# Quarter loads, packed tiles and one full-width chain in place of two interleaved chunks, in a 4:8 sparsifying kernel

One core of one Trainium2 chip. The metric is the device time of one execution in microseconds (us). Most executions of a kernel agree within some 0.3 us; a run more than 1.5% above the fastest of the same kernel is called slow. Medians below are over all runs, ratios over the fast runs only.

## The reference

```python
batch, dim = 64, 4096                      # x: float32, normal
x_flat  = x.copy().reshape(-1, 8)
indices = np.argsort(np.abs(x_flat), axis=-1)
for i in range(x_flat.shape[0]):
    x_flat[i, indices[i, :4]] = 0          # the 4 smallest of 8 become 0
```

Every value keeps itself if its magnitude is among the four largest of its group of eight. The kernel doesn't sort. It finds the fourth largest magnitude of a group with a network of minima and maxima, compares the eight magnitudes with it and multiplies by the mask.

## The kernel before

The 64 x 4096 input is laid out as 128 partitions x 2048 values, that is 256 groups of eight per partition. It goes through in two chunks of 128 groups, each with tiles of its own (two buffers), so that the scheduler can put the second chunk's instructions between the first's:

```python
for c in range(2):                                   # NCHUNK
    nc.sync.dma_start(out=x_t, in_=x_v[:, col0:col1])            # 512 KB
    nc.scalar.activation(out=a, in_=x_t, func=Abs)               # ACT
    tt(hi1, ev, od, max); tt(lo1, ev, od, min)                   # level 1, 512 values each
    tt(Q[0:2], hi1 even, hi1 odd, max); tt(mh, ..., min)         # level 2, 4 ops of 256
    tt(nl, lo1 even, lo1 odd, max);     tt(U[3:5], ..., min)
    tt(Q[2:4], mh, nl, max); tt(Q[4:6], mh, nl, min)             # the mh/nl pair
    tt(U[0:3], Q[0::2], Q[5:0:-2], min)                          # the minimum, 384
    nc.vector.tensor_reduce(t4, U, max)                          # 640 -> 128
    tt(mask, a, t4 broadcast, is_ge); tt(res, mask, x_t, mult)   # 1024 each
    nc.scalar.dma_start(out=out_v[:, col0:col1], in_=res)        # 512 KB
# (shortened: tt is nc.vector.tensor_tensor, slices without the group axis)
```

## Time and profile before

| | before |
|---|---|
| median time | 25.09 us |
| span of the profile | 23.3 us |
| VectorE (DVE) starts | 5.73 us |
| last DVE op ends | 19.82 us |
| after it, to the end of the span | 3.48 us |

The change is judged by three lengths: the head (until DVE starts), the DVE stretch and the tail (after the last DVE op). ACT is ScalarE, which computes Abs; SP is SyncE, which issues the loads and at the end waits for the stores. A transfer has landed when its completion semaphore has arrived. Two more lines of the page of the kernel before are needed below. The first is a group of instructions (line, engine, operation, output<-inputs, shapes, count | busy us, mean ns of one | idle us before). The second is a DMA issue (KB each, us from issue to landing):

```profile
L84 DVE TENSOR_TENSOR U<-Q 128x384 f32<-128x384 f32 x2 | 1.3, 626 | 0.0
...
x_t<-in_x_dram SPq DMA_DIRECT2D x2, 512.0 KB, 4.3
```

### The profile page before, as it was taken

What the parts mean: (1) busy time and instruction counts of PE and PEld (TensorE: products, weight loads), DVE (VectorE), ACT (ScalarE), POOL (GpSimd) and SP (SyncE); (2) the same over time, 40 slices, a digit from 0 to 9 for tenths busy, and PEclk for the clock granted to TensorE, in tenths of its full rate; (3) what the DMA queues carried; (4) which work ended last, traced back from release to release, by engine and by line L of the source; (5) the groups of instructions that cost most, each with busy time, mean ns of one, the idle gap of its engine ahead of it and who ended that gap; (6) DMA issues with size and microseconds to landing.
All of it is one profiled execution on the core that took longest, in us unless ns stands there. A gap on an engine that the chain in (4) does not pass through costs nothing.

```text
span 23.3 us, 77 instructions
## 1 busy us (share of the span) xinstructions
DVE 14.0 (60%) x24; ACT 3.4 (15%) x3; POOL 0.2 (1%) x4
## 2 busy tenths in 40 slices
DVE  0000000001999999999999999999999999000000
ACT  0794000097980000000000000000000000000000
POOL 3000000000000000000000000000000000000000
DMA  0014979971000000000000000069500000059700
GB/s 0 0 14 113 323 211 373 408 302 56 0 0 0 0 0 0 0 0 0 0 0 0 0 0 0 0 274 401 225 0 0 0 0 0 0 211 401 288 0 0
DMA packets 576, 2.10 MB, mean 90 GB/s; under 512 B 64, under 2 KB 64, under 8 KB 576
## 3 DMA queue, kind: packets, MB, share of 16 engines
q1 hardware_dynamic: 288, 1.05, 13.4%
q10 hardware_dynamic: 288, 1.05, 11.1%
HBM read 1.05 MB, written 1.05 MB: 90 GB/s over the span
## 4 chain that ended last, share of the span: by engine, by line
DVE 59%; DMA 17%; ACT 5%; issue 2%
DMA x_t<-in_x_dram 17%; DVE mask L104 11%; DVE res L108 10%; DVE t L99 7%; DVE hi L59 6%; DVE lo L60 5%; DVE U L84 5%; ACT a_abs L49 5%; DVE U L77 3%; DVE Q L81 3%; DVE nl L74 3%; DVE mh L71 3%; DVE Q L80 3%; DVE Q L68 2%
## 5 line engine op out<-in xcount | busy, mean ns | idle before, releaser
L59 DVE TENSOR_TENSOR hi<-a_abs 128x512 f32<-128x512 f32 x2 | 1.4, 686 | 5.7 <-ACT a_abs L49 5.7
L49 ACT ACTIVATE a_abs<-x_t 128x1024 f32<-128x1024 f32 x2 | 2.1, 1056 | 2.8 <-DMA x_t<-in_x_dram 2.8
L108 DVE TENSOR_TENSOR res<-mask,x_t 128x1024 f32<-128x1024 f32 x2 | 2.5, 1225 | 0.0
L104 DVE TENSOR_TENSOR mask<-a_abs,t 128x1024 f32<-128x1024 f32 x2 | 2.4, 1224 | 0.0
L99 DVE TENSOR_REDUCE t<-U 128x128 f32<-128x640 f32 x2 | 1.6, 818 | 0.0
L49 ACT ACT_TABLE_LOAD x1 | 1.3, 1283 | 0.7 <-PEq L125 0.7
L60 DVE TENSOR_TENSOR lo<-a_abs 128x512 f32<-128x512 f32 x2 | 1.4, 687 | 0.0
L84 DVE TENSOR_TENSOR U<-Q 128x384 f32<-128x384 f32 x2 | 1.3, 626 | 0.0
L77 DVE TENSOR_TENSOR U<-lo 128x256 f32<-128x256 f32 x2 | 0.9, 440 | 0.0
L74 DVE TENSOR_TENSOR nl<-lo 128x256 f32<-128x256 f32 x2 | 0.8, 420 | 0.0
L81 DVE TENSOR_TENSOR Q<-mh,nl 128x256 f32<-128x256 f32 x2 | 0.8, 420 | 0.0
L68 DVE TENSOR_TENSOR Q<-hi 128x256 f32<-128x256 f32 x2 | 0.8, 419 | 0.0
L71 DVE TENSOR_TENSOR mh<-hi 128x256 f32<-128x256 f32 x2 | 0.8, 419 | 0.0
L80 DVE TENSOR_TENSOR Q<-mh,nl 128x256 f32<-128x256 f32 x2 | 0.8, 418 | 0.0
L125 POOL MEMSET const-bfloat16-1.0<- 128x1 bf16 x1 | 0.1, 102 | 0.0
L125 POOL MEMSET const-uint8-127<- 128x1 uint8 x1 | 0.1, 102 | 0.0
L125 POOL MEMSET const-float32-0.0<- 128x1 f32 x1 | 0.1, 99 | 0.2 <-issue 0.2
L125 POOL MEMSET const-float32-1.0<- 128x1 f32 x1 | 0.1, 99 | 0.0
## 6 DMA issues: line engine op xcount, KB each, us to landing
x_t<-in_x_dram SPq DMA_DIRECT2D x2, 512.0 KB, 4.3
out_dram<-res ACTq DMA_DIRECT2D x2, 512.0 KB, 2.7
```

Of the source, the lines that this page charges most:

```text
L49: nc.scalar.activation(out=a.rearrange("p g e -> p (g e)"), in_=x_t.rearrange("p g e -> p (g e)"), func=mybir.ActivationFunctionType.Abs,)
L59: nc.vector.tensor_tensor(out=hi1, in0=ev, in1=od, op=ALU.max)
L60: nc.vector.tensor_tensor(out=lo1, in0=ev, in1=od, op=ALU.min)
L71: nc.vector.tensor_tensor(out=mh, in0=hi1_r[:, :, :, 0], in1=hi1_r[:, :, :, 1], op=ALU.min)
L74: nc.vector.tensor_tensor(out=nl, in0=lo1_r[:, :, :, 0], in1=lo1_r[:, :, :, 1], op=ALU.max)
L77: nc.vector.tensor_tensor(out=U[:, :, 3:5], in0=lo1_r[:, :, :, 0], in1=lo1_r[:, :, :, 1], op=ALU.min)
L80: nc.vector.tensor_tensor(out=Q[:, :, 2:4], in0=mh, in1=nl, op=ALU.max)
L81: nc.vector.tensor_tensor(out=Q[:, :, 4:6], in0=mh, in1=nl, op=ALU.min)
L84: nc.vector.tensor_tensor(out=U[:, :, 0:3], in0=Q[:, :, 0::2], in1=Q[:, :, 5:0:-2], op=ALU.min)
L99: nc.vector.tensor_reduce(out=t4, in_=U, axis=mybir.AxisListType.X, op=ALU.max)
L104: fin.tensor_tensor(out=mask, in0=a, in1=t4.to_broadcast([P, G, 8]), op=ALU.is_ge)
L108: fin.tensor_tensor(out=res, in0=mask, in1=x_t, op=ALU.mult)
```

## The change

The intent: start DVE sooner, by loading in quarters and doing Abs and level 1 on each quarter; use fewer instructions, by packing the intermediate results into 8-word groups so that level 2 takes two ops in place of four and the rest runs once on all 256 groups; shorten the last store, by splitting the output 160 to 96.

```diff
-NCHUNK = 2
+IN_SEGS = [0, 64, 128, 192, 256]
+OUT_SEGS = [0, 160, 256]
 ...
+    for g0, g1 in zip(IN_SEGS[:-1], IN_SEGS[1:]):
+        nc.sync.dma_start(out=x_t[:, g0:g1, :], in_=x_v[:, g0:g1, :])
+        nc.scalar.activation(out=a[:, g0:g1, :], in_=x_t[:, g0:g1, :], func=Abs)
+        nc.vector.tensor_tensor(out=T1[:, g0:g1, 0:4], in0=ev, in1=od, op=ALU.max)
+        nc.vector.tensor_tensor(out=T1[:, g0:g1, 4:8], in0=ev, in1=od, op=ALU.min)
+    # from here on all 256 groups at once
+    tt(QQ words 0,1,6,7, T1 even, T1 odd, max); tt(W words 0,1,6,7, ..., min)
+    tt(QQ[2:4], W[0:2], QQ[6:8], max);          tt(QQ[4:6], ..., min)
+    tt(W[3:6], QQ[0:6:2], QQ[5:0:-2], min)
+    nc.vector.tensor_reduce(out=t4, in_=W[:, :, 3:8], op=max)
+    for g0, g1 in zip(OUT_SEGS[:-1], OUT_SEGS[1:]):
+        tt(mask, a, t4 broadcast, is_ge); tt(res, mask, x_t, mult)   # one mask buffer
+        nc.scalar.dma_start(out=out_v[:, g0:g1, :], in_=res[:, g0:g1, :])
 ... (removed: the loop over two chunks shown above; long calls shortened)
```

## The prediction

> **What bounds the kernel now.** I read the page of the profile first (busy shares and slices), then the chain of work that ended last, then the timeline, which gives the start of each single instruction.
>
> The page's busy shares, and the slices of 0.58 us:
>
> ```profile
> DVE 14.0 (60%) x24; ACT 3.4 (15%) x3; POOL 0.2 (1%) x4
> ...
> DVE  0000000001999999999999999999999999000000
> ...
> DMA  0014979971000000000000000069500000059700
> ```
>
> VectorE (DVE) is busy without a break from slice 9 to slice 33. Before that it has nothing to work on; after it only a transfer runs. So there are three parts: a head until DVE starts, a solid DVE stretch, and a tail with the last store.
>
> The timeline (start, duration, engine, line) at both ends of the DVE stretch:
>
> ```profile
> 4.64 1.06 ACT L49 ACTIVATE a_abs<-x_t 128x1024 f32<-128x1024 f32 x1 [2.63 <-DMA x_t<-in_x_dram]
> 5.73 0.69 DVE L59 TENSOR_TENSOR hi<-a_abs 128x512 f32<-128x512 f32 x1 [5.73 <-ACT a_abs L49]
> 5.85 1.06 ACT L49 ACTIVATE a_abs<-x_t 128x1024 f32<-128x1024 f32 x1 [0.15 <-DMA x_t<-in_x_dram]
> ...
> 15.03 0.42 DVE L80 TENSOR_TENSOR Q<-mh,nl 128x256 f32<-128x256 f32 x1
> 15.36 0.42 DVE L81 TENSOR_TENSOR Q<-mh,nl 128x256 f32<-128x256 f32 x1
> 15.82 0.63 DVE L84 TENSOR_TENSOR U<-Q 128x384 f32<-128x384 f32 x1
> 16.48 0.82 DVE L99 TENSOR_REDUCE t<-U 128x128 f32<-128x640 f32 x1
> 17.34 1.22 DVE L104 TENSOR_TENSOR mask<-a_abs,t 128x1024 f32<-128x1024 f32 x1
> 18.59 1.23 DVE L108 TENSOR_TENSOR res<-mask,x_t 128x1024 f32<-128x1024 f32 x1
> ```
>
> Read from it:
> - Load 1 has landed at about 4.62 us, load 2 at about 5.83 us (ACT starts 0.02 us later). DVE starts at 5.73.
> - Two neighbours that don't depend on each other (L80, L81) start 0.33 apart though one lasts 0.42: they overlap by some 0.08. An op that needs the result just before it (L84, L99, L104, L108) starts 0.03 after its end. A direct dependence thus costs about 0.115 us more than independence.
> - The last DVE op ends at 19.82; the span is 23.3. The tail is 3.48 us.
>
> The DMA part of the page gives the tail its content:
>
> ```profile
> out_dram<-res ACTq DMA_DIRECT2D x2, 512.0 KB, 2.7
> ```
>
> Issue to landing is 2.7 us for 512 KB. The windows of this store show 410 and 393 GB/s where it is in full flow, so about 1.3 us is bytes and 1.4 us is fixed; another 0.75 us of the span follows the landing. The median time (25.09) is 1.79 above the span, which I take as unchanged.
>
> **What the Trainium skill says.**
> - "VectorE: DVE Perf Modes", section "The TRN2 errata": an fp32 tensor_tensor takes (N+151)/0.96 ns. The groups agree: N=256 gives 424 (measured 419 to 420), 512 gives 691 (686), 1024 gives 1224 (1224 to 1225). I use it for 768 and 1280.
> - Same page, section "The DRAIN you can't avoid": a semaphore between chained ops costs nothing extra. The trace here differs, by the 0.115 us above, and I go by the trace.
> - "SBUF — State Buffer", section "Door 1: The DMA port swizzle": lines are 16 bytes, and at least two accesses in a row should hit the same line. The trace agrees: the stride-2 reads of L68 (two hits per line) show no penalty, while L84 measures 626 ns where the formula gives 557. Its reversed input (words 5, 3, 1 of a 6-word group) makes one single hit per group of 8 values on average: 128 of them for about 70 ns, or 0.55 ns each.
> - "ScalarE: Activation LUTs", section "What ACT_TABLE_LOAD costs": 0.833 ns per element. With the measured 1056 ns for 1024 elements, a 512-element Abs is estimated at 1056 - 427 = 629 ns.
>
> **The change, part by part.**
>
> *Instructions and elements.* The DVE elements per partition are the same: 2048 for level 1, 2048 for level 2, 1024 for the mh/nl pair, 768 for the minimum, 1280 for the reduce, 4096 for mask and multiply; 11,264 in all. DVE instructions fall from 24 to 18 (8 + 2 + 2 + 1 + 1 + 4). At about 70 ns of fixed pitch (0.33 us apart less 256/0.96 = 267 ns) this saves some 0.4 us. By itself that is under 2%.
>
> *What it loses.* The two chunks were interleaved so that a chunk-1 op stood between dependent chunk-0 ops. Now there is one chain on the whole width. Direct dependences: into level 2, the pair, the minimum, the reduce, mask 1, res 1, mask 2 (it reuses the one mask buffer) and res 2: eight, against five or so exposed before (L84, L99, L104, L108 and little else). Cost about +0.4 us, eating the saving in instructions.
>
> *Layout.* W[3:6] in 8-word groups straddles two lines, QQ[0,2,4] and QQ[5,3,1] likewise: each of three ports has one single hit in each of 256 groups. One port's worth is 256 x 0.55 = 140 ns; the ports overlap partly, so I choose +200 ns: 768 elements cost 957 + 200 = 1.16 us, against two at 0.626 before. The reduce (5 words starting at word 3) has one single hit per group; I choose +50 ns on 1333 + 152 = 1485 ns. The pair writes to words 0-1 and 6-7 sit whole in a line and cost nothing extra.
>
> *The head: where the gain is.* Before, DVE's 5.73 to 19.82 is all work. Now level 1 (8 ops, 0.34 apart, 2.7 us) runs as quarter loads of 256 KB land, most of it before the last byte is in. The last quarter should land when load 2 did, 5.85: same bytes, same queue, four issues of some 0.42 from 0.73 on are all out by 2.4. Then Abs 0.63 to 6.48, two level-1 ops 0.34 apart and 0.42 long, end at 7.26. For that the earlier quarters must be worked off: landings 0.65 to 0.7 apart (256 KB at some 400 GB/s) against 0.68 us of DVE and less than that of ACT; they just fit.
>
> *The chain from there* (start of the next = start + duration + 0.03 if dependent, - 0.08 if not):
>
>     7.29  level-2 max, 1024 elements, 1.224, next independent
>     8.43  level-2 min, 1.224
>     9.68  pair max, 512, 0.686, next independent
>     10.29 pair min, 0.686
>     11.00 minimum, 768, 1.16
>     12.19 reduce, 1280, 1.535
>     13.76 mask 1, 1280, 1.49
>     15.28 res 1, 1.49
>     16.80 mask 2, 768, 0.957
>     17.79 res 2, 0.957, ends 18.75
>
> So DVE ends 1.07 us earlier than 19.82.
>
> *The tail.* The last store falls from 512 to 384 KB: 128 KB at 410 GB/s is 0.31 us less, 3.17 in place of 3.48. The first store (640 KB) is issued at about 16.8 and has its bytes moved by about 19.0, before those of the second, so the two don't collide. Span 18.75 + 3.17 = 21.9, time 21.9 + 1.79 = **23.7 us**, 5.5% less.
>
> **Rivals.**
> 1. *The loads stretch.* Quarters have rows of 2 KB in place of 4 KB and twice the issues. Against it: the loads move 434 GB/s in their best half microsecond, a rate with room. For it: the first load needs 3.9 us where a store of the same size needs 2.7, so the start is slow in a way that I don't understand, and DVE's first dependent full-width op waits for the very last byte. Each 0.1 us of later landing costs 0.1. If the last quarter lands at 6.4: 24.2.
> 2. *Full width undoes the overlap.* Level 2 can't start before 7.3, where it started at 6.94 on half the data before. If the landings bunch (all within a microsecond) ACT and DVE queue up: four Abs and eight level-1 ops behind a first landing of 4.4 give a level-1 end of 7.4 to 7.6, +0.15 to +0.35: 23.9 to 24.1.
> 3. *False dependences.* If slices of one tile were tracked as the whole tile, load 2 would wait for Abs 1, and so on: several microseconds slower. Against it: L80 and L81 write interleaved slices of one Q without a wait, 0.33 apart. I give it 2%.
> 4. *Strides cost less or more.* If hits are averaged over a line buffer, minimum and reduce lose 0.25 us: 23.45. If the three ports' penalties add, 0.2 more: 23.9.
> 5. *No gain but bookkeeping*: fewer instructions against more dependences cancel. They do in my sum; what is left is the work moved into the head (level 1 under the loads, 1.07 in all) and the shorter store (0.31). For "within 2%" (over 24.59) 0.9 us of this would have to fail.
>
> **Range and chances.** The terms with width are the last landing (-0.2 to +0.5), the strides (-0.25 to +0.2), the bunching (0 to 0.3) and the tail (0.15 either way). Taken as independent they give about 23.3 to 24.2 for 8 in 10, a little wider above. Faster by over 2% means below 24.59, which only a sum of bad terms or rival 3 misses: 0.93. Within 2%: 0.05. Slower: 0.02.
>
> **What would show it.** Right: DVE with 18 ops; last Abs starting at 5.7 to 6.0; level-2 max at 7.2 to 7.5 with no gaps over 0.05 us after it; minimum at 1.1 to 1.2 us; res 2 ending near 18.7; the last store landing 2.4 us after its issue. Wrong on the loads: the last Abs over 6.2. Wrong on bunching: DVE busy without idle from first to last level-1 op and level 2 late though the last Abs is on time. Wrong on strides: minimum near 0.96 or above 1.3, reduce near 1.49 or above 1.6. The prediction as a whole fails if the DVE end isn't about a microsecond earlier.

## The result

The changed kernel takes 24.26 us (median of 11 runs, 24.24 to 24.67) against 25.09 (16 runs). The ratio of the fast runs is 0.968 (95% interval 0.9656 to 0.9705). A ratio here is the mean time of one kernel's fast runs over that of the other's of the same rounds, so it is not quite the ratio of the medians. The change is faster, by 3.2%; 5.5% was forecast, and 24.26 lies just above the range.

| us | before | predicted | after |
|---|---|---|---|
| DVE starts | 5.73 | - | 4.73 |
| last Abs starts | 5.85 | 5.85 | 6.32 |
| level-2 max starts | - | 7.29 | 7.78 |
| last DVE op ends | 19.82 | 18.75 | 19.13 |
| tail | 3.48 | 3.17 | 3.35 |
| span | 23.30 | 21.9 | 22.48 |
| time | 25.09 | 23.7 | 24.26 |

The page of the changed kernel, busy time and slices:

```profile
DVE 14.0 (62%) x18; ACT 3.8 (17%) x5; POOL 0.2 (1%) x4
...
DVE  0000000059997999999999999999999999000000
```

DVE is busy for 14.0 us with 18 instructions, exactly as long as with 24 before. The bookkeeping of fewer instructions gave nothing in busy time. What changed is where the stretch lies: it begins in slice 8 and is not quite full there. The timeline of the changed kernel (start, duration):

```profile
4.07 2.01 ACT L49 ACTIVATE a_abs<-x_t 128x512 f32<-128x512 f32 x3 [2.06 <-DMA x_t<-in_x_dram]
4.73 0.42 DVE L56 TENSOR_TENSOR T<-a_abs 128x256 f32<-128x256 f32 x1 [4.73 <-ACT a_abs L49]
...
6.32 0.63 ACT L49 ACTIVATE a_abs<-x_t 128x512 f32<-128x512 f32 x1 [0.24 <-DMA x_t<-in_x_dram]
...
7.33 0.42 DVE L57 TENSOR_TENSOR T<-a_abs 128x256 f32<-128x256 f32 x1
7.78 1.23 DVE L62 TENSOR_TENSOR QQ<-T 128x1024 f32<-128x1024 f32 x1
...
18.17 0.96 DVE L91 TENSOR_TENSOR res<-mask,x_t 128x768 f32<-128x768 f32 x1
```

The first quarter has landed at 4.05, the last at 6.30; level 2 needs both level-1 ops of the last quarter and starts at 7.78. DVE starts 1.00 us earlier than before, its stretch (4.73 to 19.13) is 14.40 us against 14.09, so it ends 0.69 earlier. (The Abs of a quarter takes 630 ns, as the 629 that the prediction estimated.) The chain of work that ended last (start, duration, what) goes back through that last load:

```profile
1.62 0.42 SPq L48
2.04 0.04 issue
2.08 4.22 DMA x_t<-in_x_dram
```

SyncE (SP) issues the four loads one after the other, each 0.36 to 0.43 us; the fourth starts at 2.08 and ends at 2.52. The groups for the two strided ops, and the stores:

```profile
L78 DVE TENSOR_REDUCE t<-W 128x256 f32<-128x1280 f32 x1 | 1.5, 1487 | 0.0
...
L75 DVE TENSOR_TENSOR W<-QQ 128x768 f32<-128x768 f32 x1 | 1.1, 1071 | 0.0
...
out_dram<-res ACTq DMA_DIRECT2D x1, 384.0 KB, 2.5
```

The minimum pays 114 ns over the formula's 957 where I had put 200, the reduce pays nothing where I had put 50. The last store lands 2.5 us after its issue, not the 2.4 that 0.31 less than 2.7 would be.

### The profile page after: what moved, and what is told of

It is laid out like the page before. It is cut to its first block, busy times and chain, and to the rows that moved or that the text cites. A ratio compares the mean times of both kernels' runs of the same rounds, so it can differ in the third digit from the quotient of the medians.

```text
span 22.5 us, 77 instructions
## 1 busy us (share of the span) xinstructions
DVE 14.0 (62%) x18; ACT 3.8 (17%) x5; POOL 0.2 (1%) x4
## 4 chain that ended last, share of the span: by engine, by line
DVE 53%; DMA 19%; SPq 5%; ACT 3%; issue 2%
DMA x_t<-in_x_dram 19%; DVE mask L85 11%; DVE res L91 11%; DVE t L78 7%; DVE QQ L62 5%; SPq L48 5%; DVE W L66 5%; DVE W L75 5%; DVE QQ L72 3%; ACT a_abs L49 3%; DVE QQ L73 3%; DVE T L56 2%; DVE T L57 2%
## 5 line engine op out<-in xcount | busy, mean ns | idle before, releaser
L56 DVE TENSOR_TENSOR T<-a_abs 128x256 f32<-128x256 f32 x4 | 1.7, 426 | 4.8 <-ACT a_abs L49 4.7
L49 ACT ACTIVATE a_abs<-x_t 128x512 f32<-128x512 f32 x4 | 2.5, 630 | 2.4 <-DMA x_t<-in_x_dram 2.3
L91 DVE TENSOR_TENSOR res<-mask,x_t 128x1280 f32<-128x1280 f32 (+1 forms) x2 | 2.5, 1225 | 0.1
L85 DVE TENSOR_TENSOR mask<-a_abs,t 128x1280 f32<-128x1280 f32 (+1 forms) x2 | 2.4, 1224 | 0.1
L57 DVE TENSOR_TENSOR T<-a_abs 128x256 f32<-128x256 f32 x4 | 1.7, 419 | 0.0
L78 DVE TENSOR_REDUCE t<-W 128x256 f32<-128x1280 f32 x1 | 1.5, 1487 | 0.0
L62 DVE TENSOR_TENSOR QQ<-T 128x1024 f32<-128x1024 f32 x1 | 1.2, 1225 | 0.0
L66 DVE TENSOR_TENSOR W<-T 128x1024 f32<-128x1024 f32 x1 | 1.2, 1218 | 0.0
L75 DVE TENSOR_TENSOR W<-QQ 128x768 f32<-128x768 f32 x1 | 1.1, 1071 | 0.0
L72 DVE TENSOR_TENSOR QQ<-W,QQ 128x512 f32<-128x512 f32 x1 | 0.7, 692 | 0.0
L73 DVE TENSOR_TENSOR QQ<-W,QQ 128x512 f32<-128x512 f32 x1 | 0.7, 683 | 0.0
```

Of the source, the lines that this page charges most:

```text
L49: nc.scalar.activation(out=a[:, g0:g1, :], in_=x_t[:, g0:g1, :], func=mybir.ActivationFunctionType.Abs,)
L56: nc.vector.tensor_tensor(out=T1[:, g0:g1, 0:4], in0=ev, in1=od, op=ALU.max)
L57: nc.vector.tensor_tensor(out=T1[:, g0:g1, 4:8], in0=ev, in1=od, op=ALU.min)
L62: nc.vector.tensor_tensor(out=QQ_r[:, :, 0::3, :], in0=l2_in0, in1=l2_in1, op=ALU.max)
L66: nc.vector.tensor_tensor(out=W_r[:, :, 0::3, :], in0=l2_in0, in1=l2_in1, op=ALU.min)
L72: nc.vector.tensor_tensor(out=QQ[:, :, 2:4], in0=mh, in1=nl, op=ALU.max)
```

## The experiments

Unless said otherwise an experiment is the changed kernel with the edit shown, its result is correct, and "before" was run in the same rounds (25.04 to 25.09 us in median).

My theory after the result: the head decides. Level 2 (the first step on the whole width) starts when the last quarter has landed, or when DVE has got through eight level-1 ops from the first landing on, whichever is later. Both landings came later than I had assumed, and the tail gave back part of the shorter store. Rivals: the late landing is an accident of one profile; it comes from 2 KB rows and not from four serial issues; it is the fewer instructions or the layout that carry the gain, not the quarters; the order of the ops doesn't matter.

### Is the profile typical? e0_after and e16_after_again

Edit: none.

> The changed kernel itself once more, as the reference for its neighbours on this chip and as a second look at its landings: time 24.26, first Abs near 4.07, last Abs near 6.32, DVE end near 19.13 and 3.3 to 3.4 us of tail. If the late last landing was an accident of one profile, it comes back to about 5.9 here.

> The changed kernel: 24.0 to 24.4, DVE end 19.1 to 19.2 in the profiled run.

Measured: 24.24 us (ratio 0.9636, 0.958 to 0.9692) and 24.27 us (ratio 0.9635, 0.9595 to 0.9676). In these two profiles the first Abs starts at 3.90 and 3.91, DVE ends at 19.16 and 19.26, the tail is 3.3 to 3.4. The late landing is no accident: the trace has the last Abs at 6.35 and 6.39. Eleven profiles have the same four quarter loads; their last landings lie at 6.14 to 6.47 (6.67 in e6, a slow run), those of the three with two loads of 512 KB in 4 KB rows (before, e1, e11) at 5.77 to 5.85. But landings move from run to run, and here the second quarter came late (Abs at 4.93 and 5.10 in place of 4.77), so that DVE stood idle for 0.27 and 0.43 before it. In e16 that sets the start of level 2 (7.90): from the second quarter on DVE has no gap. So a middle piece can bind as well as the first and the last. The end is the same within 0.13 us.

### Do the quarters carry the gain? e11_halves

```diff
-IN_SEGS = [0, 64, 128, 192, 256]
+IN_SEGS = [0, 128, 256]
```

> The changed kernel with loads, Abs and level 1 in two halves in place of four quarters; the rest unchanged. This undoes the one part that I hold to carry the gain. Theory: DVE starts at 5.73 as before the change, level 1 ends near 8.2, DVE ends near 19.6, time near 24.7: most of the gain is gone, and the rest is the shorter last store. Rival (the gain comes from fewer instructions or from the layout): the time stays near 24.3.

Measured: 24.71 us, ratio 0.9881 (0.9853 to 0.9909). The timeline:

```profile
5.74 0.69 DVE L56 TENSOR_TENSOR T<-a_abs 128x512 f32<-128x512 f32 x1 [5.74 <-ACT a_abs L49]
...
8.29 1.23 DVE L62 TENSOR_TENSOR QQ<-T 128x1024 f32<-128x1024 f32 x1
```

DVE starts when it did before (5.74); its last op starts at 18.69, lasts 0.96 and ends at 19.65, 0.17 us before the kernel before. So packing, full width and the 18 instructions, less their exposed dependences, give 0.17 us at DVE's end. With the shorter tail that is 1.2% in time. The quarters give the other 2%: they move level 2 from 8.29 to 7.78.

### Why does the last quarter land late? e1 to e4

These four change only how the bytes are fetched; Abs and level 1 stay in quarters.

e1_two_loads:

```diff
-    four loads of [:, g0:g1, :], 64 groups each
+    for g0, g1 in ((0, 128), (128, 256)):
+        nc.sync.dma_start(out=x_t[:, g0:g1, :], in_=x_v[:, g0:g1, :])
```

> The changed kernel with two loads of 512 KB (4 KB rows) in place of four of 256 KB; Abs and level 1 stay in quarters. Both theories for the late last landing (6.30 us after the change, 5.83 before) expect it to come back to about 5.83: (A) four serial issues of 0.42 us put the last load's start back, (B) 2 KB rows are served slower per byte. Since two Abs quarters then wait for that one landing, level 2 should start at 5.85 + 0.53 + 0.63 + 0.78 = about 7.8, as after the change (7.78), and the time stays near 24.3. If the landing stays at 6.3, neither theory holds (the level-1 reads or the Abs would have to disturb the load).

e2_two_loads_2kb:

```diff
+    x_s  = x_t.rearrange("p (s g) e -> p s g e", s=4)     # x_vs likewise
+    for s0 in (0, 1):
+        nc.sync.dma_start(out=x_s[:, s0::2, :, :], in_=x_vs[:, s0::2, :, :])
```

> Two issues of 512 KB, but in runs of 2 KB (load 1 brings quarters 0 and 2, load 2 quarters 1 and 3). A (number of issues): last landing near 5.85, time near 24.3. B (row size): last landing near 6.3, level 2 near 8.25, time near 24.7.

e3_two_queues:

```diff
+    for i, (g0, g1) in enumerate(zip(IN_SEGS[:-1], IN_SEGS[1:])):
+        q = nc.sync if i % 2 == 0 else nc.scalar
+        q.dma_start(out=x_t[:, g0:g1, :], in_=x_v[:, g0:g1, :])
```

> The changed kernel with its four quarter loads issued in turn from SP and from ACT, so that the fourth issue starts at about 1.15 us in place of 2.08. A: last landing near 5.85, level 2 near 7.3, time near 23.8. B: last landing stays near 6.3 and the time near 24.26. If ACT's table load (1.28 us) goes behind its two issues it ends near 2.9, before the first landing, and costs nothing.

e4_four_loads_4kb:

```diff
+    for g0, g1 in ((0, 128), (128, 256)):
+        for p0 in (0, 1):
+            nc.sync.dma_start(out=x_t[p0::2, g0:g1, :], in_=x_v[p0::2, g0:g1, :])
```

> Four issues of 256 KB from SP, but with rows of 4 KB: every second partition of one half each. A: last landing stays near 6.3, and since two Abs quarters wait for it, level 2 near 8.25, time near 24.7. B: last landing near 5.85, level 2 near 7.8, time near 24.3.

Measured (landings are the times of the last completion semaphore of each load in the traces):

| run | issues | rows | last issue, start to end | last landing | time | ratio to before |
|---|---|---|---|---|---|---|
| before | 2 | 4 KB | 1.15 to 1.57 | 5.83 | 25.09 | 1 |
| after | 4 on SP | 2 KB | 2.08 to 2.52 | 6.30 | 24.26 | 0.968 |
| e1 | 2 | 4 KB | 1.14 to 1.57 | 5.77 | 24.59 | 0.9808 (0.977 to 0.9847) |
| e2 | 2, 0.6 us each | 2 KB | 1.40 to 2.00 | 6.41 | 26.06; two of four runs slow, the fast ones 25.68 and 25.74 | none given |
| e3 | 4 on SP and ACT | 2 KB | 1.16 to 1.62 | 5.98 | 24.34 | 0.972 (0.967 to 0.977) |
| e4 | 4 on SP, 0.5 to 0.6 each | 4 KB | 2.57 to 3.16 | 6.54 | 26.04 | 1.037 (1.0314 to 1.0427) |

e3 is the telling one: the same four loads with the same 2 KB rows end 0.32 us sooner when two queues issue them side by side. e4, with rows of 4 KB but four issues in series, lands late. Both point to serial issue. But e3 changes two things, when the loads are issued and how many queues carry them, and the traces speak against the issue times as the cause. These are two stretches of the loads, in the kernel before, the changed one and e3 (the last number is GB/s, the one before it the busy share of the DMA engines). Before:

```profile
1.50:3.75 2.25, 0.00 (x0) 0.51 (x1) 0.00 (x0) 1.00 0.76 213
3.75:5.25 1.50, 0.00 (x0) 0.61 (x1) 0.00 (x0) 1.00 0.89 358
```

After:

```profile
1.50:3.75 2.25, 0.00 (x0) 0.51 (x1) 0.00 (x0) 1.00 0.73 207
3.75:5.25 1.50, 0.52 (x2) 1.11 (x2) 0.00 (x0) 1.00 0.87 305
```

e3:

```profile
1.50:3.75 2.25, 0.00 (x0) 1.28 (x1) 0.00 (x0) 1.00 0.63 185
3.75:5.25 1.50, 0.05 (x1) 0.71 (x2) 0.00 (x0) 1.00 1.04 397
```

Up to 3.75 us the changed kernel moved its bytes as fast as the kernel before (207 and 213 GB/s), and faster than e3. It lost its time afterwards, at 305 GB/s against 358 and 397, though its last issue had ended at 2.52. Two more runs don't fit issue times either: e2, whose two issues ended at 2.00, landed at 6.41, and e15 (below), with four serial issues at the same times as the changed kernel but pieces of other sizes, at 5.97. So what is shown is that issuing on two queues brings back 0.32 of the 0.47 (5.98 lies below all eleven landings of the same loads on one queue). Whether one queue is slower here because of the 2 KB rows, of the number of transfers on it or of something else, no run separates.

e1 landed where both theories had it, but level 2 started at 8.06 and not at 7.8, and its time was 24.59 and not 24.3. Its first landing, at 4.57, let DVE start at 5.25, and from there it was busy with level 1 without a gap. The next run shows the same.

And yet e3 isn't faster. Its timeline:

```profile
4.54 2.38 ACT L51 ACTIVATE a_abs<-x_t 128x512 f32<-128x512 f32 x4 [1.60 <-DMA x_t<-in_x_dram]
5.20 0.43 DVE L58 TENSOR_TENSOR T<-a_abs 128x256 f32<-128x256 f32 x1 [5.20 <-ACT a_abs L51]
...
8.01 1.23 DVE L64 TENSOR_TENSOR QQ<-T 128x1024 f32<-128x1024 f32 x1
```

The loads issued side by side arrive side by side, the first two at 4.51 and 4.70, where the changed kernel has its first at 4.05. DVE starts at 5.20 and needs until 8.0 for its eight level-1 ops without any gap. This is the second bound: had the last quarter of the changed kernel landed at 5.83, DVE, starting at 4.73, would still have been at level 1 until 4.73 + 7 x 0.34 + 0.42 = 7.53. Of the 0.49 us that level 2 came late, a punctual last landing would have given back some 0.2.

e2 and e4 missed their times by more than a microsecond, for reasons that I had overlooked. In e2, ACT takes the quarters in order, so the third quarter, which came with the first load, waited behind the second, which came with the second. In e4 each Abs needs two loads, and its first wait was placed ahead of ACT's table load. The chain of waits shows the table load on the path, from 4.75 to 6.03:

```profile
4.75 1.28 ACT L51
```

### What does a direct dependence cost? e5_mask_own_buffer

```diff
-        mask = pool.tile([P, OUT_SEGS[1], 8], dt, name="mask")
+        mask = pool.tile([P, n, 8], dt, name=f"mask{g0}")
```

> The second mask gets a buffer of its own; the order becomes mask 1, mask 2, res 1, res 2, so that three direct dependences go (mask 2 on res 1, res 1 on mask 1, res 2 on mask 2). Theory (a dependence on the op just before costs some 0.115 us): DVE ends 0.35 us earlier, near 18.8. Rival (a semaphore between chained ops costs nothing, as the Trainium skill's page VectorE: DVE Perf Modes says): DVE end stays near 19.13. The first store is issued about 0.8 us later, near 18.0, so its bytes run to about 20.4 and push the last store's back by some 0.4: the time should gain little or nothing, 24.2 to 24.4.

Measured: 24.61 us, ratio 0.9825 (0.9785 to 0.9864). The end of its timeline:

```profile
14.13 2.36 DVE L85 TENSOR_TENSOR mask<-a_abs,t 128x1280 f32<-128x1280 f32 x2
16.41 2.35 DVE L91 TENSOR_TENSOR res<-mask,x_t 128x1280 f32<-128x1280 f32 x2
```

Mask 1 starts at 14.13 as in the changed kernel, and DVE ends at 18.76 in place of 19.13: three dependences less, 0.37 us less, 0.12 each. Up to that point the chain runs as in the changed kernel. What depends on an op two places back no longer costs anything visible: the two masks and the two products overlap as independent ops do (1.49 + 0.96 us in 2.36). The time got worse, because the first store leaves at 17.93 in place of 17.18 and the last one, now issued only 0.87 us after it, lands 3.3 us after its issue in place of 2.5. That I had expected to cost 0.4; it cost 0.8.

### Where did the shorter store's gain go? e6, e8, e12

e6_out_half:

```diff
-OUT_SEGS = [0, 160, 256]
+OUT_SEGS = [0, 128, 256]
```

> Only the stores change: 128 and 128 groups in place of 160 and 96. DVE end stays near 19.13. Tail: if the extra 0.18 us that the changed kernel spends between the last store's bytes and the wait's end comes from 3 KB rows or from the first store's nearness, it goes away, the tail is 3.48 as before the change and the time about 24.35; if it is in the changed kernel whatever the store, the tail is 3.6 or more and the time 24.5.

Measured: 24.49 us, ratio 0.975 (0.9708 to 0.9791). The profiled run was a slow one (its second quarter and third came late and DVE ended at 19.55), but its stores land 2.7 us after their issue, as before the change, and its tail is 3.45. That is the tail of the first reading (3.48); the time, expected at 24.35 with it, came out above, with fast runs of 24.34 to 24.53.

e8_out_96:

```diff
-OUT_SEGS = [0, 160, 256]
+OUT_SEGS = [0, 96, 256]      # the mask buffer stays at 160 groups
```

> The changed kernel with its stores the other way round: 96 groups first (384 KB in rows of 3 KB), 160 last. In all runs so far the wait for a last store of 384 KB ended 0.58 to 0.64 us after its last packet, for stores of 512 or 640 KB 0.36 to 0.43. If that goes with the 3 KB rows, the first store's landing is the long one here (2.5 us from its issue) and the 640 KB store's is 3.0; the tail after the last DVE op is then 3.48 + 0.31 = 3.8, time near 24.8. If it goes with being the last store after another, the last store takes 3.2 and the first 2.3.

Measured: one look, 24.87 us. The DMA lines are those of the changed kernel, 640 KB in 3.0 us and 384 KB in 2.5 us, though the 384 KB store is now the first and alone in flight; the tail is 3.78, as expected. So its slow landing goes with its shape, not with its place.

e12_store_4kb_rows:

```diff
+OUT_SEGS = [0, 128, 256]
+        if g0 == 0:
+            nc.scalar.dma_start(out=out_v[0::2, g0:g1, :], in_=res[0::2, g0:g1, :])
+        # the odd partitions of this half are stored after the last store
```

> As e6 (stores at 128 and 128 groups), but the first store takes every second partition only: 256 KB in rows of 4 KB, alone in flight; the other half of it is stored after the last store. A store of 256 KB in rows of 2 KB took 2.56 us from issue to the end of the wait, 0.77 of it after its last packet; 512 KB in rows of 4 KB takes 2.7, 0.39 of it after. Floor: this store takes about 2.55 us as well. Rows: it takes 2.7 - 0.62 = 2.1 us, plus up to 0.15 for the longer issue of a stepped pattern. The kernel's own time says nothing here (a third store follows, about 25.5).

Measured: one look, 24.98 us. The DMA view of the window from 15 to 18 us has this store alone:

```profile
out_dram<-res ACTq DMA_DIRECT2D x1, 256.0 KB, 2.4
```

From the traces' packet records and the end of SP's wait for each store (in e10 the two stores overlap, and which packet was the first one's last is uncertain by some 0.1):

```
store             rows   us from its last packet to the end of the wait
512 KB (before)   4 KB   0.40, 0.43
640 KB (after)    5 KB   0.43
384 KB (after)    3 KB   0.60
384 KB (e8)       3 KB   0.57
256 KB (e10)      2 KB   0.87, 0.77
256 KB (e12)      4 KB   0.43
```

In the changed kernel the last packet of the 384 KB store comes 1.97 us after its issue, against 2.28 for 512 KB: 0.31 less, as predicted. But the wait then ends 0.60 us later in place of 0.43. The lag goes with the length of the rows and not with the bytes, since 256 KB in rows of 4 KB has the lag of 512 KB in such rows. Why short rows are confirmed late, no run here shows. e12 took 2.43 us where the row theory had 2.25 at most. Its stepped pattern made the issue 0.18 us longer (0.55 us), which leaves some 0.15 over 2.1; a small part of a floor may be in it as well.

### Does the stride cost come from the output? e9_min_inside_line

```diff
-        out=W[:, :, 3:6], in0=QQ[:, :, 0:6:2], in1=QQ[:, :, 5:0:-2], op=ALU.min
+        out=W[:, :, 4:7], in0=QQ[:, :, 0:6:2], in1=QQ[:, :, 5:0:-2], op=ALU.min
+    nc.gpsimd.memset(W[:, :, 3:4], 0.0)      # at the start
```

> The minimum writes words 4 to 6 of each group in place of 3 to 5, so that its output no longer straddles a 16-byte line (a wrong result on purpose; word 3 is cleared at the start by GpSimd so that nothing unset is read). It took 1071 ns, 114 over the 957 of the formula. If the output's straddling costs, it falls to 957 to 1020; if the inputs' single hits set it, it stays at 1071. Everything else, the time too, is as after the change (24.3).

Measured: one look, 24.34 us, result wrong as intended. The group:

```profile
L76 DVE TENSOR_TENSOR W<-QQ 128x768 f32<-128x768 f32 x1 | 1.1, 1073 | 0.0
```

1073 against 1071 ns: where the output lies makes no difference. The 114 ns, or 0.45 ns per group, are left to the two inputs; which of them, no run tells. By the prediction's count only the reversed input makes single hits in the kernel before, and L84 pays 626 - 557 = 69 ns on 128 groups, 0.54 each. By that count a second such input adds nothing here.

### Does the order of the ops matter? e7, e13, e10

e7_interleaved: quarters up to level 1, then two halves whose ops stand between each other (two stores of 128 groups, one mask tile of 256 groups).

```diff
-    # chain on all 256 groups
+    l1(q0); l1(q1); l2max(A); l2min(A); l1(q2); pmax(A); pmin(A); l1(q3); umin(A)
+    l2max(B); l2min(B); red(A); pmax(B); pmin(B); ge(A); umin(B); mul(A); store(A)
+    red(B); ge(B); mul(B); store(B)          # A, B: 128 groups each
```

> Quarter loads, Abs and level 1 as changed, then everything in two halves whose ops stand between each other as before the change (24 DVE instructions, stores of 128 and 128 groups; its control is e6). Theory (full width pays for the fewer instructions with exposed dependences and with a wait for the last load): DVE starts at 4.73, has 11.73 of elements + 24 x 0.07 + two exposed dependences + 0.2 of strides and last latency = 13.85, so it ends near 18.6, and the time is near 23.8, half a microsecond under e6. Rival (DVE work alone counts, the order doesn't): 6 more instructions make it end 0.4 later than e6, time near 24.8.

Measured: 24.13 us, ratio 0.9605 (0.9547 to 0.9663), against 24.49 and 0.975 for its control e6: 0.36 us better with six instructions more, so the rival falls. Against the changed kernel of the same rounds (24.24, 0.9636) it is no clear gain. And DVE ends at 18.99 and not at 18.6:

```profile
5.57 0.42 DVE L65 TENSOR_TENSOR T<-a_abs 128x256 f32<-128x256 f32 x1 [0.15 <-ACT a_abs L56]
...
6.52 0.43 DVE L65 TENSOR_TENSOR T<-a_abs 128x256 f32<-128x256 f32 x1 [0.19 <-ACT a_abs L56]
...
17.76 1.23 DVE L93 TENSOR_TENSOR res<-mask,x_t 128x1024 f32<-128x1024 f32 x1
```

It stood idle twice, 0.15 and 0.19 us, for the Abs of quarters that had just landed.

e13_interleaved_a_first, against e7:

```diff
-    l2max(A); l2min(A); l1(q2)
+    l2max(A); last = l2min(A)
+    for i in l1(q2): ...      # ordered after `last` by an edge that makes no wait
```

> e7 with one difference: level 2 of half A comes before level 1 of the third quarter, as in e10, but with two stores of 512 KB as in e7. If the wait for the third quarter's Abs (0.19 us in e7) is saved, DVE ends near 18.8 and the time is near 23.95; if the second quarter's landing takes it back, as in e10 (idle 0.20 before it), the time is that of e7, 24.1.

Measured: 24.19 us, ratio 0.9668 (0.9601 to 0.9735), the same as e7 within the intervals. The 0.19 went, but DVE now stood 0.43 us before the second quarter, whose Abs started at 5.08 in this run. The landings take back what the order gives.

e10_three_stores, against e13:

```diff
-    ge(B); mul(B); store(B)
+    ge(B1); ge(B2); mul(B1); store(B1); mul(B2); store(B2)      # 64 groups each
```

> The interleaved version e7, with level 2 of half A placed before the level 1 of the third quarter (no wait for its Abs, 0.19 in e7), and with the last half's mask and multiply cut in two and stored separately (256 KB each; mask 1, mask 2, res 1, res 2, no exposed dependence between them). Theory: DVE ends near 18.99 - 0.19 - 0.12 + 0.14 = 18.8; the tail of a 256 KB store is 3.41 - 0.62 = 2.8, or 3.0 if its receipt is longer; span 21.6 to 21.8, time 23.4 to 23.6. Rival (the landings, not the order, hold DVE): DVE end stays at 19.0 and the time at 23.7 to 23.8.

Measured: 24.11 us, ratio 0.9616 (0.9582 to 0.965), no better than e7, half a microsecond above what I expected. DVE ends at 18.97 (idle 0.20 before the second quarter). The tail is 3.6 us and not 2.8. The DMA line of the page for its last two stores:

```profile
out_dram<-res ACTq DMA_DIRECT2D x2, 256.0 KB, 2.6
```

Half the bytes in half-length rows land almost as late.

### Can DVE start earlier, and does the end follow? e14, e15

e14_small_first:

```diff
-IN_SEGS = [0, 64, 128, 192, 256]
+IN_SEGS = [0, 32, 96, 176, 256]
```

> The changed kernel with loads of 128, 256, 320 and 320 KB in place of four of 256. If the first landing (3.2 to 3.3 us after its issue) follows its bytes, the first Abs starts 0.3 earlier, at about 3.65, and takes 0.2 less, so DVE starts near 4.1; if it is start-up latency, the first Abs still starts at 3.9 to 4.0 and DVE near 4.4. Level 2 waits for the last landing and the Abs of 80 groups (0.13 longer, and level 1 of it 0.17 longer): time 24.3 to 24.5 in either case, no gain.

Measured: 24.26 us in median, but of four runs two are slow (24.49, 24.75); the two fast ones (24.0, 24.04) give 0.9589 (0.9532 to 0.9646). Two fast runs are few, so I don't claim a gain. The profiled run is one of the slow ones. Its first landing is clear all the same:

```profile
3.61 0.29 DVE L56 TENSOR_TENSOR T<-a_abs 128x128 f32<-128x128 f32 x1 [3.61 <-ACT a_abs L49]
...
5.36 0.43 DVE L56 TENSOR_TENSOR T<-a_abs 128x256 f32<-128x256 f32 x1 [1.26 <-ACT a_abs L49]
```

The first Abs starts at 3.16, earlier than either reading had it (3.65, or 3.9 to 4.0). A first load of 128 KB lands 2.3 to 2.4 us after its issue (e14, e15), one of 256 KB 3.1 to 3.4, and the difference is more than bytes alone at 400 GB/s would make (0.33). DVE starts 1.1 us sooner and then has nothing to do for 1.26 us.

e15_small_chunk_first fills that gap: the first 32 groups go through all steps up to their threshold before the second quarter's Abs is there, and their mask and multiply stand later between dependent ops of the others. Edges that make no wait fix the order of all DVE ops.

```diff
+IN_SEGS = [0, 32, 96, 176, 256]      # OUT_SEGS as changed: 160, 96
+    l1(q0); l2max(A); l2min(A); pmax(A); pmin(A); umin(A); red(A)     # A: 32 groups
+    l1(q1); l1(q2); l1(q3)
+    l2max(B); l2min(B); pmax(B); pmin(B); umin(B); ge(A); red(B); mul(A)  # B: 224
+    ge(B1); mul(B1); store(0, 160); ge(B2); mul(B2); store(160, 256)
```

> Loads of 128, 256, 320 and 320 KB as in e14; the first 32 groups go through everything up to their threshold (8 small ops, about 2 us with their dependences) in the gap before the second quarter's Abs; then level 1 of the rest, the chain on 224 groups in full width, with the mask and multiply of the 32 groups between its dependent ops; stores as in the changed kernel (160 and 96 groups). Theory (DVE's gap-free start sets the end): DVE starts at 3.6, idles little before 5.4 to 5.6, then has 10.8 us of elements, 18 x 0.07 and some 0.8 of dependences, strides and last latency: it ends near 18.4 and the time is 23.5 to 23.7. Rival (the last landing and full width hold it): level 2 of the 224 groups starts at 8.0 as in e14, DVE ends near 18.9 and the time is 24.0 to 24.1.

Measured: 23.49 us, ratio 0.9357 (0.9335 to 0.9378), against 24.27 and 0.9635 for the changed kernel in the same rounds. Four of its six runs lie at 23.47 to 23.49, two at 24.03 and 24.06 count as slow. It beats both kernels. The span of its profile is 21.7 us. Its timeline:

```profile
3.53 0.49 DVE L53 TENSOR_TENSOR T<-a_abs 128x128 f32<-128x128 f32 x2 [3.53 <-ACT a_abs L68]
...
5.53 2.36 DVE L53 TENSOR_TENSOR T<-a_abs 128x256 f32<-128x256 f32 x6
...
17.39 0.96 DVE L53 TENSOR_TENSOR res<-mask,x_t 128x768 f32<-128x768 f32 x1
```

DVE works from 3.53 on, is at the second quarter at 5.53 and never waits for a load again; it ends at 18.35 (18.4 expected), with the tail of the changed kernel. It is busy for 14.5 us, half a microsecond more than in either kernel, and is still done sooner: this work lies in the head, where DVE had nothing else to do.

## Why the prediction was wrong, step by step

The direction and the mechanism held: level 1 under the loads and a shorter last store. Two terms of the sum were too good, and two others made up for a little.

- **"The last quarter should land when load 2 did, 5.85"** is the step that failed. It landed at 6.30, 0.45 us later, in a profile that two repeats confirm; by the prediction's own sign (last Abs over 6.2; it started at 6.32) it was wrong on the loads. "Same bytes, same queue" didn't give the same rate: 305 GB/s from 3.75 to 5.25 us against 358 before. "All out by 2.4" was nearly right (2.52), and the traces speak against the issue times as the reason. Issuing on two queues (e3) brought the landing back to 5.98; why one queue is slower with these loads stays open. My first rival named this case with its price (6.4: 24.2 us); I gave it too little weight.
- **"They just fit"** failed as well. Landings 0.65 to 0.7 apart that end at 5.85 mean a first landing at 3.75 to 3.9; it came at 4.05, and DVE started at 4.73. For level 2 at 7.29 it would have had to start its eight level-1 ops by about 4.5. e1 and e3 show this bound by itself.
- My second rival had this bound, but its sum was too short. Behind a first landing of 4.4, an Abs of 0.63 and eight level-1 ops (7 x 0.34 + 0.42) end at about 7.87, and not at 7.4 to 7.6. e3 agrees with the mended sum: landing 4.51, last level-1 op ending at 7.97.
- Together these put level 2 at 7.78 in place of 7.29: 0.49 us, the larger part of the 0.56 by which the time missed.
- **The chain from there** was right within 0.11: 11.35 us from level 2 to the end where I had 11.46. The dependence cost held (0.03 after the end, 0.12 each by e5). The strides were a little too dear: 1071 and 1487 ns where I had 1160 and 1535.
- **"The last store falls by 0.31 us"**: its last packet did, but the landing is confirmed 0.17 us later with rows of 3 KB, and the tail shrank by 0.13 only.
- "Saves some 0.4 us" in instructions and "eating the saving" in dependences: they cancel in busy time (14.0 us both times). e11, without the quarters, ends DVE 0.17 earlier than before.
- The sum of the errors: 0.49 - 0.11 + 0.18 (tail, 3.35 for 3.17) = 0.56, less 0.01 because the time lies 1.78 over the span here and not 1.79: 0.55. The time missed by 24.26 - 23.7 = 0.56. The range gave the last landing half a microsecond of room, but as one term among independent ones and with no term for the tail's shape, so its upper end of 24.2 was just too low.

## What to carry to other kernels

When a load is cut so that work can start sooner, write down a landing time for every piece. The first sets when the engine starts; for each piece, its landing plus the work still to be done from it on is a bound on when the first whole-width op can run (here the first, the second and the last quarter each came to bind). Don't take the landing of the last piece from a load of other size and number (6.30 for 5.85). The gap that an early small piece opens was clearly worth something once a whole chunk of the chain filled it (e15: 2.9% under the changed kernel by the ratios of the same rounds); without that, e14 leaves it open. Interleave chunks where ops depend on the op just before (0.12 us each here), and don't expect a last store of half the bytes to land in half the time if its rows get shorter (2.6 us for 256 KB, 2.7 for 512).

## What the Trainium skill lacked or had wrong

- "VectorE: DVE Perf Modes", section "The DRAIN you can't avoid", has it that a semaphore between chained ops costs nothing extra, measured on eight `tensor_copy`. Here a dependence on the op just before does cost: three of them less moved DVE's end from 19.13 to 18.76 us, 0.12 us each (e5).
- "Vector Engine (DVE) Microarchitecture Reference", section "5.2 Measured stream behaviour on trn2 (trn3 not measured)", says that a port runs at full rate only on runs of at least two adjacent words. Here stride-2 inputs, which have no adjacent words, run at full rate: level 2 takes 1225 and 1218 ns for 1024 values where the formula of contiguous operands gives 1224. The 16-byte line that the prediction used fits better. The minimum, with a single hit per group on each port, paid 114 ns in 256 groups, and moving its output inside a line changed nothing (1071 and 1073 ns).
- "DMA: Bandwidth & Descriptors", section "Issuing engines are not separate DMA queues", has it that issuing on several engines "will only save the time on the sequencer". Here issuing the same four loads on two queues ended them 0.32 us sooner (e3), though it had moved fewer bytes by 3.75 us: the gain came after all issues were out, at 397 GB/s against 305.
- I found no page that gives how late a store is confirmed by the length of its rows: 0.40 to 0.43 us after the last packet for rows of 4 and 5 KB, 0.57 to 0.60 for 3 KB, 0.77 to some 0.9 for 2 KB.
